# Two-layer hybrid decoder trunk: position tables called one block earlier, stream sums one block later, the last tile's matmuls in two pieces of columns

## The chip, the core and the metric

One core of one Trainium2 chip runs the whole program as one launch. The metric is the device time in microseconds; a comparison on the chip takes the median over several executions. Each engine works through its own queue of instructions in the order in which the program was built, and waits at an instruction until the semaphores that it names are reached. PE is the matrix engine, DVE the vector engine, ACT the scalar engine, POOL the general engine, SP the engine whose queue issues most DMAs.

## The reference, cut to what matters

```python
for l in range(2):                                   # h is (256 tokens, 1024)
    h = h + 0.5 * swiglu(rmsnorm(h, ffn1_norm[l]), ffn1_w_gate[l], ffn1_w_up[l], ffn1_w_down[l])
    u = rmsnorm(h, mix_norm[l])
    z = u @ w_in[l]                                  # latent attention | differential attention | pooling | gates
    ...                                              # three mixers; RoPE and ALiBi use `positions`
    h = h + merged @ w_out[l]
    h = h + 0.5 * swiglu(rmsnorm(h, ffn2_norm[l]), ffn2_w_gate[l], ffn2_w_up[l], ffn2_w_down[l])
return rmsnorm(h, final_norm)
```

`swiglu` is `(silu(x @ w_gate) * (x @ w_up)) @ w_down` with an inner width of 2816. All is float32.

## The kernel before

**Products.** A float32 product is made of three products of rounded parts: every operand is split into `hi` (rounded) and `lo` (the rest), and `mm3` issues hi·hi, hi·lo and lo·hi into one PSUM tile (lines 212 to 214; the second one, line 213, is the first that needs `lo` of the weights). Weights come in tiles of 128 x 4 x 512 (1 MB) by DMAs from SP's queue into five `raw` buffers. ACT casts a tile to `hi` (line 194), DVE subtracts to get `lo` (line 195), each into three buffers; a `raw` buffer is free for the next DMA when its `lo` is done. PE uses a weight tile in 24 matmuls of 512 columns: 4 slices of k, 2 token tiles `t`, 3 parts.

**A feed-forward stage** (`ffn`) walks over the inner width in blocks of 512 columns, c = 0, 512, 1024, 1536, 2048, 2560. A block has a gate half (m = 0) and an up half (m = 1), each of two weight tiles. Counted from 0, weight tiles 0 to 3 belong to block 0, tiles 4 and 5 to the gate half and 6 and 7 to the up half of block 512, 8 to 11 to block 1024, 12 to 15 to block 1536. `turned` transposes the product of the block before (line 428) between the gate and the up half. One block of each stage (c = 2048 in the first stage, 1536 in the three others; `sevens`) is done with seven products instead of eight (`Seven`). It needs sums and differences of the activations, made on DVE and ACT by `stream` (lines 240 to 250), and differences of weights, made on DVE by `sums` (line 258).

**Position tables.** `tables` makes the RoPE and ALiBi tables once, in the first stage. POOL writes a token value into two tiles, `pi` and `pr` (lines 525, 526), which ties the two DMAs behind it to the product `g` that is handed over; then ACT's queue issues the DMAs (lines 527, 528): `pi` gathers 256 single integers, two per partition, `pr` copies the same 1 KB row to 128 partitions. DVE turns them into `ndist` and `ang` (lines 536 to 569), ACT into sines. A third DMA, `lr` (line 578), reuses the buffer of `pr`. The tables are first read in the mixing stage.

**The end.** In the last stage `gemm_tokens` is called with `tail=2`: the last two weight tiles of w_down are done for token tile 0 first and then for token tile 1. For each token tile, `last_half` then adds to h (line 500), squares (ACT, 952), multiplies with the norm's weights (954), takes the power -1/2 on POOL (959), scales columns 0 to 511 on DVE (960) and 512 to 1023 on ACT (962), and stores them by a DMA of SP's and one of ACT's queue.

The order on each engine is set by a scheduler of the framework when the program is built, and the framework puts in the semaphore waits: for data, for buffers, and for tiles that overlap.

Of the kernel before, what the change touches and what calls it, by code (L numbers as in the profile page):

```python
# [11 lines left out]
F32 = mybir.dt.float32  # L12
# [3 lines left out]
AF = mybir.ActivationFunctionType  # L16
# [80 lines left out]
def trunk(ctx, tc, x, xt, positions, wall, small, lamrow, fnorm, out):  # L97
# [110 lines left out]
            split(slice(k, k + step))  # L208
        return hi, lo

    def mm3(ps, lh, ll, rh, rl, start, stop):
        nc.tensor.matmul(ps, lhsT=lh, rhs=rh, start=start, stop=False)  # L212
        nc.tensor.matmul(ps, lhsT=lh, rhs=rl, start=False, stop=False)  # L213
        nc.tensor.matmul(ps, lhsT=ll, rhs=rh, start=False, stop=stop)  # L214

    flat = lambda a: a.rearrange("p k n -> p (k n)")

# [97 lines left out]
            add(c21, c, m1)  # L315
            return (a, u2), (c21, m5)

    def gemm_tokens(specs, xh, xl, n, before=None, tail=1, early=None):

        ps = [acc(), acc()]
        last = specs[-1][2] + specs[-1][3] - 1
        parts = [[s] for s in specs[:-tail]] + [specs[-tail:]]
        for part in parts:
            w = [(s[2] + j, hi[:, j, :], lo[:, j, :]) for s in part for hi, lo in (wsplit(s),) for j in range(s[3])]
            if before and part is parts[-1]:
                before()
# [5 lines left out]
            for k, wh, wl, t in order:  # L334
                tk = slice(t * P, (t + 1) * P)
                mm3(ps[t][:, :n], xh(k)[:, tk], xl(k)[:, tk], wh, wl, k == 0, k == last)
        return ps

    def rsqrt_mean(dst, src, n):
# [4 lines left out]
    class Norm:  # L344
# [73 lines left out]
    def ffn(l, pre, u, following, midway=None):  # L418
# [18 lines left out]
        pending = None  # L437
        for c in range(0, DFF, 512):
            n = min(512, DFF - c)
            if c == 1024 and midway:  # L440
                midway(g[0][:, :2])
            spec = lambda b, k: (f"{pre}_gu", l, k, 4, b, 512)
            if c == 0:

                ps = [[b() for _ in range(2)] for b in (acc, trp)]
                for k0 in (0, 4):
                    for m in range(2):
                        wh, wl = wsplit(spec(m * 512, k0))
# [10 lines left out]
                if sevens(l, pre)[0] == 1024:  # L459
                    seven.stream(u.hi, u.lo)  # L460
            elif c in sevens(l, pre):
                rows = seven.run(lambda: turned(*pending))
                ps = [[rows[t][m] for t in range(2)] for m in range(2)]
            elif n == 512:
                ps = []
                if c + 512 in sevens(l, pre):
                    at = 2 * c + 1024
                    last = latest[0]
                    seven.sums([spec(at, 0), spec(at + 512, 0), spec(at + 512, 4), spec(at, 4)])
                    latest[0] = last  # L470
                for m in range(2):
                    ps.append(gemm_tokens([spec(2 * c + m * 512, k) for k in (0, 4)], u.xh, u.xl, 512))
# [19 lines left out]
            pending = c, g  # L492
        nxt = following() if following else None
        for half in range(2):
            pd = gemm_tokens([(f"{pre}_w_down", l, k, min(4, KF - k), half * 512, 512) for k in range(0, KF, 4)],
                             lambda k: ghi[k // 8][:, k % 8, :], lambda k: glo[k // 8][:, k % 8, :], 512,
                             tail=1 if nxt else 2, early=(lambda: turned(*pending)) if half == 0 else None)
            for t in range(2):
                hs = h[:, t, half * 512:(half + 1) * 512]
                nc.vector.scalar_tensor_tensor(out=hs, in0=pd[t], scalar=0.5, in1=hs, op0=ALU.mult, op1=ALU.add)  # L500
            if nxt:
                nxt.half(half)
            elif l == DEPTH - 1 and pre == "ffn2":
                last_half(half)
        return nxt


# [430 lines left out]

    hf = {}

    def last_half(n):
        if n == 0:
            hf["fn"] = big([P, D], F32, "fn")
            nc.scalar.dma_start(out=hf["fn"], in_=fnorm.broadcast_to([P, D]))
            hf["ss"] = sp.tile([P, 2, 2], F32, tag="ss", name="ss", bufs=2)
            hf["o"] = big([P, 2, D], F32, "of")
            hf["r"] = sp.tile([P, 2], F32, tag="r", name="r", bufs=2)
        ss, o, r = hf["ss"], hf["o"], hf["r"]
        ns = slice(n * 512, (n + 1) * 512)
        for t in range(2):  # L950
            sq = tp.tile([P, 512], F32, tag="C", name="sq")
            nc.scalar.activation(out=sq, in_=h[:, t, ns], func=AF.Square, accum_out=ss[:, n, t:t + 1])
            rt, s_ = r[:, t:t + 1], ss[:, n, t:t + 1]
            nc.vector.tensor_tensor(out=o[:, t, ns], in0=h[:, t, ns], in1=hf["fn"][:, ns], op=ALU.mult)
            if n == 0:
                nc.vector.tensor_scalar(out=rt, in0=s_, scalar1=1.0 / D, scalar2=EPS, op0=ALU.mult, op1=ALU.add)
                continue
            nc.vector.scalar_tensor_tensor(out=rt, in0=s_, scalar=1.0 / D, in1=rt, op0=ALU.mult, op1=ALU.add)
            nc.gpsimd.tensor_tensor(out=rt, in0=rt, in1=mhalf[:, :1], op=ALU.pow)
            nc.vector.tensor_scalar(out=o[:, t, :512], in0=o[:, t, :512], scalar1=rt, scalar2=None, op0=ALU.mult)  # L960
            nc.sync.dma_start(out=out[t * P:(t + 1) * P, :512], in_=o[:, t, :512])
            nc.scalar.activation(out=o[:, t, 512:], in_=o[:, t, 512:], func=AF.Identity, scale=rt)
            nc.scalar.dma_start(out=out[t * P:(t + 1) * P, 512:], in_=o[:, t, 512:])

    u = Norm(0, SM_F1)
    u.first(0)
# [71 lines left out]
```

## Time and profile before

| | |
|---|---|
| median of 3 runs (lowest to highest) | 1209.01 us (1208.99 to 1210.8) |
| the profiled execution's own time | 1208.78 us |
| its span, first to last instruction | 1207.0 us |
| PE busy | 1193.4 us (99%) |
| DVE / ACT / POOL busy | 818.9 (68%) / 603.4 (50%) / 68.2 us (6%) |
[...]
| chain that ended last | PE 88%, DVE 5%, issue 4%, DMA 2% |

The profiled execution lies 0.23 us under the median, and its time 1.78 us over its span. A matmul's record is longer than the distance to the next one, since matmuls are pipelined: distances are read from start to start. In a timeline row the first two numbers are start and duration in microseconds, and the brackets say how long the engine had been idle before and what released it.

### The profile page before, as it was taken

How to read it: one execution, taken by the hardware profiler on the slowest of the kernel's cores; microseconds unless marked ns; L12 is line 12 of the kernel's file. 1: busy time of each engine (PE TensorE's matmuls, PEld its weight loads, DVE VectorE, ACT ScalarE, POOL GpSimd, SP SyncE). 2: the span in 40 equal slices, each digit the busy share in tenths (PEclk: the TensorE clock that was granted, in tenths of full speed). 3: DMA queues.
4: the chain of work that ended last, by engine and by line, in shares of the span. 5: the costliest groups of instructions: out<-in, count | busy, mean ns of one | idle time of the engine just before them, and what ended most of it. 6: DMA issues, size and time to landing. Idle time of an engine off the chain costs nothing.

```text
span 1207.0 us, 14974 instructions
## 1 busy us (share of the span) xinstructions
PE 1193.4 (99%) x5944; PEld 999.8 (83%) x5944; DVE 818.9 (68%) x1124; ACT 603.4 (50%) x792; POOL 68.2 (6%) x126
## 2 busy tenths in 40 slices
PE   9999999999999999999999999999999999999997
PEld 7878889997788888888888888899877888888886
DVE  6789646777757658963558964568686485599553
ACT  6456444545644455643445643455455445446432
POOL 0000000600100000000000000034010000000000
PEclk9999999999999999999999999999999999999999
DMA  9645545235455554655554565544433554545540
GB/s 338 261 179 177 213 166 204 83 136 179 140 174 180 176 201 141 211 193 186 184 204 172 176 225 175 179 148 147 146 137 140 177 205 170 180 175 211 177 153 35
DMA packets 35478, 212.86 MB, mean 176 GB/s; under 512 B 4177, under 2 KB 5585, under 8 KB 12113
## 3 DMA queue, kind: packets, MB, share of 16 engines
q1 hardware_dynamic: 34272, 210.52, 49.8%
q10 hardware_dynamic: 1136, 1.40, 0.4%
q8 instruction: 46, 0.75, 0.2%
q14 instruction: 24, 0.19, 0.0%
HBM read 210.85 MB, written 1.05 MB: 176 GB/s over the span
## 4 chain that ended last, share of the span: by engine, by line
PE 88%; DVE 5%; issue 4%; DMA 2%; ACT 1%; POOL 0%; SPq 0%; POOLq 0%; ACTq 0%; DVEq 0%
PE acc L212 24%; PE acc L213 23%; PE acc L214 23%; PE acc L278 6%; PE o L772 2%; PE tr L428 1%; DVE lo L195 1%; PE tr L738 1%; PE tr L765 1%; PE tr L214 1%; PE tr L212 1%; PE tr L213 1%; PE tr L727 1%; DMA raw<-wall 1%; PE tr L359 1%
## 5 line engine op out<-in xcount | busy, mean ns | idle before, releaser
L195 DVE TENSOR_TENSOR lo<-raw,hi 128x1024 fp32r<-128x1024 f32 (+4 forms) x274 | 428.9, 1580 | 281.9 <-ACT hi L194 281.7
L194 ACT CAST hi<-raw 128x1024 fp32r<-128x1024 f32 (+4 forms) x274 | 358.0, 1330 | 375.3 <-PE acc L214 274.4
L212 PE MATMUL acc<-hi,uhi 128*128 128x512 f32 (+1 forms) x768 | 300.9, 392 | 0.5 <-DVE uhi L376 0.5
L213 PE MATMUL acc<-lo,uhi 128*128 128x512 f32 (+1 forms) x768 | 299.0, 389 | 2.3 <-DVE lo L195 2.3
L214 PE MATMUL acc<-hi,ulo 128*128 128x512 f32 (+1 forms) x768 | 298.2, 389 | 0.4 <-DVE ulo L377 0.4
L213 PEld LDWEIGHTS acc<-lo,uhi 128*128 128x128 f32 x768 | 144.3, 188 | 31.1 <-DVE lo L195 2.7
L212 PEld LDWEIGHTS acc<-hi,uhi 128*128 128x128 f32 x768 | 144.0, 188 | 30.0 <-issue 2.2
L214 PEld LDWEIGHTS acc<-hi,ulo 128*128 128x128 f32 x768 | 144.1, 188 | 29.4 <-DVE ulo L377 1.0
L212 PE MATMUL acc<-hi,ghi 128*128 128x512 f32 x352 | 137.7, 391 | 0.0
L213 PE MATMUL acc<-lo,ghi 128*128 128x512 f32 x352 | 137.4, 390 | 0.0
L214 PE MATMUL acc<-hi,glo 128*128 128x512 f32 x352 | 137.3, 390 | 0.0
L212 PEld LDWEIGHTS acc<-hi,ghi 128*128 128x128 f32 x352 | 66.1, 188 | 13.8
L214 PEld LDWEIGHTS acc<-hi,glo 128*128 128x128 f32 x352 | 66.1, 188 | 13.6
L213 PEld LDWEIGHTS acc<-lo,ghi 128*128 128x128 f32 x352 | 66.1, 188 | 13.4
L757 ACT ACTIVATE e<-e,mx 128x128 f32<-128x128 f32 (+1 forms) x96 | 42.7, 446 | 56.0 <-DVE mx L753 34.1
L212 PE MATMUL acc<-uhi,hi 128*128 128x256 f32 x192 | 55.6, 290 | 0.0
L213 PE MATMUL acc<-ulo,hi 128*128 128x256 f32 x192 | 55.2, 288 | 0.0
L214 PE MATMUL acc<-uhi,lo 128*128 128x256 f32 x192 | 55.0, 288 | 0.0
L342 POOL TENSOR_TENSOR r<-r,mhalf 128x2 f32<-128x2 f32 x6 | 4.2, 701 | 699.8 <-DVE r L341 699.8
L222 ACT CAST hi<-raw 128x2048 fp32r<-128x2048 f32 x16 | 30.8, 1923 | 20.8 <-PE acc L214 19.9
L488 ACT ACTIVATE sg<-acc,r 128x512 f32<-128x512 f32 (+1 forms) x44 | 28.4, 652 | 24.6 <-PE acc L214 24.5
L212 PE MATMUL acc<-hi,y 128*128 128x512 f32 x96 | 37.8, 393 | 0.0
(236 smaller groups left out, 1639.6 us busy)
## 6 DMA issues: line engine op xcount, KB each, us to landing
raw<-wall SPq DMA_DIRECT2D x182, 1024.0 KB, 4.9
raw<-wall SPq DMA_DIRECT2D x26, 256.0 KB, 5.4
raw<-wall SPq DMA_DIRECT2D x10, 512.0 KB, 3.6
raw<-wall SPq DMA_DIRECT2D x4, 832.0 KB, 4.4
raw<-wall SPq DMA_DIRECT2D x2, 768.0 KB, 4.3
xT<-xt SPq DMA_DIRECT2D x8, 128.0 KB, 4.3
h<-x SPq DMA_DIRECT2D x4, 256.0 KB, 5.9
fn<-fnorm ACTq DMA_DIRECT2D x1, 512.0 KB, 4.8
```

The source lines that it names most:

```text
L194: nc.scalar.copy(out=hif[:, ks], in_=rawf[:, ks])
L195: nc.vector.tensor_tensor(out=lof[:, ks], in0=rawf[:, ks], in1=hif[:, ks].bitcast(F32), op=ALU.subtract)
L212: nc.tensor.matmul(ps, lhsT=lh, rhs=rh, start=start, stop=False)
L213: nc.tensor.matmul(ps, lhsT=lh, rhs=rl, start=False, stop=False)
L214: nc.tensor.matmul(ps, lhsT=ll, rhs=rh, start=False, stop=stop)
L222: nc.scalar.copy(out=flat(hi), in_=flat(x))
L278: nc.tensor.matmul(ps, lhsT=x, rhs=y, start=not onto and k == 0 and n == 0, stop=k == 3 and n == 2, skip_group_check=onto)
L359: nc.tensor.transpose(out=ps[:, (i * 2 + t) * P:(i * 2 + t + 1) * P], in_=h[:, t, k * P:(k + 1) * P], identity=ident)
L428: nc.tensor.transpose(out=ptr[:, (i * 2 + t) * P:(i * 2 + t + 1) * P], in_=g[t][:, (j + i) * P:(j + i + 1) * P], identity=ident)
L488: nc.scalar.activation(out=sg, in_=ps[0][t], func=AF.Silu, scale=r)
L757: nc.scalar.activation(out=e[:, sl], in_=e[:, sl], func=AF.Exp, bias=mx[:, i:i + 1], scale=-(2.0 ** -(hd + 1)) if slope else -1.0, accum_o ...
L772: nc.tensor.matmul(o[:, hd * 64:(hd + 1) * 64], lhsT=eT[:, j * P:(j + 1) * P], rhs=v[:, kt, hd * 64:(hd + 1) * 64], start=(kt == 0), stop= ...
```

## The change

Three edits. `tables` is called at the start of block 512 and not of block 1024, so that it hangs on the product of block 0. In the first stage `stream` is called in block 1024 and not in block 512 (`c + 1024 == sevens(l, pre)[0]`; in the other stages this is block 512 as before). And in the last half of the last stage, the final two weight tiles are done as three pieces: token tile 0 with 512 columns, token tile 1 with columns 0 to 255, then token tile 1 with columns 256 to 511; `done` is called after each, so that the addition to h, the squares and the multiplication follow each piece. The scaling of the output is cut at column 640 instead of 512.

```diff
-    def gemm_tokens(specs, xh, xl, n, before=None, tail=1, early=None):
+    def gemm_tokens(specs, xh, xl, n, before=None, tail=1, early=None, done=None):
...
-        last = specs[-1][2] + specs[-1][3] - 1
+        ends = [specs[-1][2] + specs[-1][3] - 1] + ([specs[-tail][2] - 1] if done else [])
...
+            if part is parts[-1] and done:
+                pieces = [(0, slice(0, n)), (1, slice(0, n // 2)), (1, slice(n // 2, n))]
+            else:
+                pieces = [(None, slice(0, n))]
+            for piece, cols in pieces:
+                for k, wh, wl, t in order:
+                    if piece in (None, t):
+                        tk = slice(t * P, (t + 1) * P)
+                        mm3(ps[t][:, cols], xh(k)[:, tk], xl(k)[:, tk], wh[:, cols], wl[:, cols], k == 0,
+                            k in ends, piece is not None)
+                if piece is not None:
+                    done(ps[piece], piece, cols)
...
-            if c == 1024 and midway:
+            if c == 512 and midway:
                 midway(g[0][:, :2])
...
-                        if c == 512 and not seven.sh:
+                        if c + 1024 == sevens(l, pre)[0]:
                             seven.stream(u.hi, u.lo)
...
+            def added(bank, t, cols):
+                hs = h[:, t, half * 512 + cols.start:half * 512 + cols.stop]
+                nc.vector.scalar_tensor_tensor(out=hs, in0=bank[:, cols], scalar=0.5, in1=hs, op0=ALU.mult, op1=ALU.add)
+
+            def ended(bank, t, cols):
+                added(bank, t, cols)
+                last_piece(t, half * 512 + cols.start, half * 512 + cols.stop)
...
+    def last_piece(t, c0, c1):
...
+        sq = tp.tile([P, 512], F32, tag="C", name="sq")
+        nc.scalar.activation(out=sq[:, :c1 - c0], in_=h[:, t, c0:c1], func=AF.Square, accum_out=s_)
+        nc.vector.tensor_tensor(out=o[:, t, c0:c1], in0=h[:, t, c0:c1], in1=hf["fn"][:, c0:c1], op=ALU.mult)
...
+        if c1 == D:
             nc.gpsimd.tensor_tensor(out=rt, in0=rt, in1=mhalf[:, :1], op=ALU.pow)
...
+            cut = 640
+            nc.vector.tensor_scalar(out=o[:, t, :cut], in0=o[:, t, :cut], scalar1=rt, scalar2=None, op0=ALU.mult)
+            nc.sync.dma_start(out=out[t * P:(t + 1) * P, :cut], in_=o[:, t, :cut])
+            nc.scalar.activation(out=o[:, t, cut:], in_=o[:, t, cut:], func=AF.Identity, scale=rt)
+            nc.scalar.dma_start(out=out[t * P:(t + 1) * P, cut:], in_=o[:, t, cut:])
```

**ACT's queue in block 512.** In the kernel before, these rows stand there: the last two of the four casts of weight tile 5 (128x512 each), the whole casts of weight tiles 6 and 7 (128x2048), a Silu, and the cast of weight tile 8.

```order
L194 CAST hi<-raw 128x512 [waits DMAHW3_49]
L194 CAST hi<-raw 128x512 [waits DMAHW4_49]
L194 CAST hi<-raw 128x2048 [waits DMAHW5_49,DVE_49,PE_49]
L194 CAST hi<-raw 128x2048 [waits DMAHW6_49,DVE_49,PE_49]
L488 ACTIVATE sg<-acc,r 128x512 [waits DVE_49,PE_49]
L194 CAST hi<-raw 128x2048 [waits DMAHW7_49,DVE_49,PE_49]
```

In the changed kernel the same place reads:

```order
L194 CAST hi<-raw 128x512 [waits DMAHW3_49]
L194 CAST hi<-raw 128x512 [waits DMAHW4_49]
L544 DMA pi<-positions 128x2x1 [waits Pool_49]
L545 DMA pr<-positions 128x256 [waits Pool_49]
L194 CAST hi<-raw 128x2048 [waits DMAHW5_49,DVE_49,PE_49]
L595 DMA lr<-lamrow 128x256 [waits DMAHW7_49,DVE_49]
L194 CAST hi<-raw 128x2048 [waits DMAHW0_49,PE_49,Activation_49]
L496 ACTIVATE sg<-acc,r 128x512 [waits PE_49]
L194 CAST hi<-raw 128x2048 [waits DMAHW1_49,PE_49,Activation_49]
```

The two position DMAs now stand ahead of the cast of weight tile 6, and the `lr` DMA, which waits for `pr` to land and for DVE to have read it, ahead of the cast of weight tile 7.

**DVE's queue in block 512.** In the kernel before, the products `g` of block 0, the last two pieces of `lo` of weight tile 5 and the `lo` of weight tiles 6 to 8 follow one another:

```order
L490 SCALAR_TENSOR_TENSOR g<-tr,r,sg 128x512 x2
L195 TENSOR_TENSOR lo<-raw,hi 128x512 x2
L195 TENSOR_TENSOR lo<-raw,hi 128x2048 x3
```

In the changed kernel, from the last two pieces of weight tile 5 to the `lo` of weight tile 6 (the rows for `ci`, `pf` and `cf` read `pi`; those for `ri` read `pr`):

```order
L571 CAST pf<-pi 128x2
L555 CAST cf<-ci 128x4
L575 TENSOR_SCALAR ang<-sm,pf 128x16 x2
L553 TENSOR_SCALAR ri<-pr 128x256
L554 TENSOR_SCALAR ri<-pr 128x256
L577 TENSOR_SCALAR kk<-ang 128x32
L555 CAST rf<-ri 128x512
L579 TENSOR_SCALAR kk<-kk 128x32
...
L562 SCALAR_TENSOR_TENSOR ndist<-part 128x256
L561 TENSOR_TENSOR part<-part 128x256
L584 SCALAR_TENSOR_TENSOR ang<-kk,ang 128x32
L195 TENSOR_TENSOR lo<-raw,hi 128x2048
```

From `ri` on, thirteen table operations stand ahead of the `lo` of weight tile 6 (the dots stand for five more `part` rows); there were none.

**PE's queue at the end.** In the changed kernel the last matmul of the piece with columns 0 to 255 and the first of the piece with columns 256 to 511 (both of token tile 1, in one PSUM tile) read:

```order
L214 MATMUL acc<-hi,glo 128x256
L212 MATMUL acc<-hi,ghi 128x256 [waits DVE_49]
L213 MATMUL acc<-lo,ghi 128x256
L214 MATMUL acc<-hi,glo 128x256
L212 MATMUL acc<-hi,ghi 128x256
```

The wait for DVE is new. It goes away when the addition to h after the first column piece is left out, so it is the wait for that addition, which reads the other half of the same PSUM tile. On DVE that addition stands here:

```order
L969 TENSOR_TENSOR of<-h,fn 128x512
L973 SCALAR_TENSOR_TENSOR r<-ss_9209,r 128x1
L977 TENSOR_SCALAR of<-of,r 128x640
L505 SCALAR_TENSOR_TENSOR h<-acc,h 128x256
L969 TENSOR_TENSOR of<-h,fn 128x256
```

It is the fourth row, behind the output scaling of token tile 0 (`of`, 640 columns).

## Rows read from the trace of the kernel before

**Rows 1.** Who waited for whom, PE: us in total, times, longest.

```profile
PE acc L213 <- DVE lo L195: 2.3, 1, 2.3
```

**Rows 2.** Timeline of PE, weight tile 6 and weight tile 13.

```profile
41.28 0.39 PE L213 MATMUL acc<-lo,uhi 128*128 128x512 f32 x1
41.50 0.39 PE L214 MATMUL acc<-hi,ulo 128*128 128x512 f32 x1
...
82.69 0.50 PE L213 MATMUL acc<-lo,uhi 128*128 128x512 f32 x1 [2.27 <-DVE lo L195]
```

**Rows 3.** Timeline of DVE in the first stage.

```profile
29.47 1.41 DVE L490 SCALAR_TENSOR_TENSOR g<-tr,r,sg 128x512 f32<-128x512 f32 x2
30.79 1.29 DVE L195 TENSOR_TENSOR lo<-raw,hi 128x512 fp32r<-128x512 f32 x2
32.44 2.29 DVE L195 TENSOR_TENSOR lo<-raw,hi 128x2048 fp32r<-128x2048 f32 x1 [0.36 <-ACT hi L194]
...
59.15 0.29 DVE L536 TENSOR_SCALAR ri<-pr 128x256 int32<-128x256 int32 x1 [2.41 <-DMA pr<-positions]
...
61.90 0.42 DVE L538 CAST rf<-ri 128x512 f32<-128x512 int32 x1
...
62.38 0.35 DVE L540 TENSOR_SCALAR part<-rf,cf 128x256 f32<-128x256 f32 x1
...
64.43 0.38 DVE L558 TENSOR_SCALAR ang<-sm,pf 128x16 f32<-128x16 f32 x1
...
80.35 4.48 DVE L195 TENSOR_TENSOR lo<-raw,hi 128x2048 fp32r<-128x2048 f32 x2
```

**Rows 4.** Chain that ended last, 53 to 60 us: start, us, what.

```profile
53.47 5.59 DMA pr<-positions
```

**Rows 5.** Timeline of POOL and of ACT, first stage.

```profile
50.65 0.58 POOL L525 COPY pi<-g 128x2 int32<-128x2 int32 x1 [26.54 <-DVE g L490]
...
51.26 0.39 ACTq L527 DMA_DIRECT2D pi<-positions  x1
...
68.94 1.28 ACT L488 ACT_TABLE_LOAD   x1
```

**Rows 6.** DMA issues in 20 to 100 us: KB, us to landing.

```profile
lr<-lamrow ACTq DMA_DIRECT2D x1, 128.0 KB, 3.0
pi<-positions ACTq DMA_DIRECT2D x1, 1.0 KB, 2.1
```

**Rows 7.** DMA queues (packets, MB, share): 55.5 to 58.5, 52 to 53.2, 31.95 to 39.7 us.

```profile
q1 hardware_dynamic: 121, 0.87, 71.7%
q10 hardware_dynamic: 142, 0.13, 15.4%
...
q10 hardware_dynamic: 272, 0.00, 10.5%
...
q1 hardware_dynamic: 450, 3.29, 101.6%
```

**Rows 8.** Timeline of DVE and ACT at the end.

```profile
1198.66 0.49 DVE L960 TENSOR_SCALAR of<-of,r 128x512 f32<-128x512 f32 x1 [0.66 <-POOL r L959]
...
1200.43 0.69 DVE L500 SCALAR_TENSOR_TENSOR h<-acc,h 128x512 f32<-128x512 f32 x1 [1.28 <-PE acc L214]
...
1202.74 0.72 ACT L962 ACTIVATE of<-of,r 128x512 f32<-128x512 f32 x1 [0.86 <-POOL r L959]
...
1203.49 0.35 ACTq L963 DMA_DIRECT2D out<-of  x1
```

**Rows 9.** Instructions of tiles g and sq: ns min/median/max, forms.

```profile
L490 DVE SCALAR_TENSOR_TENSOR g<-acc,r,sg x32: 476/745/751, 49.8 to 1140.6; 128x512 f32<-128x512 f32 x24, 128x256 f32<-128x256 f32 x8
...
L614 ACT ACTIVATE sq<-acc x8: 276/332/385, 201.2 to 800.6; 128x256 f32<-128x256 f32 x4, 128x128 f32<-128x128 f32 x4
```

**Rows 10.** Timeline of PE, matmuls of 256 columns in the mixing stage.

```profile
203.72 0.28 PE L213 MATMUL acc<-ulo,hi 128*128 128x256 f32 x1
203.83 0.28 PE L214 MATMUL acc<-uhi,lo 128*128 128x256 f32 x1
```

More of the change, by code (lines that the diff above doesn't have):

```diff
@@ L209, in wsplit_now, with mm3 @@
         return hi, lo
[L211 to L214, printed above, removed]
+    def mm3(ps, lh, ll, rh, rl, start, stop, onto=False):
+        nc.tensor.matmul(ps, lhsT=lh, rhs=rh, start=start, stop=False, skip_group_check=onto)
+        nc.tensor.matmul(ps, lhsT=lh, rhs=rl, start=False, stop=False, skip_group_check=onto)
+        nc.tensor.matmul(ps, lhsT=ll, rhs=rh, start=False, stop=stop, skip_group_check=onto)
     flat = lambda a: a.rearrange("p k n -> p (k n)")
@@ L333, in gemm_tokens @@
                 order.sort(key=lambda o: o[3])
-            for k, wh, wl, t in order:
-                tk = slice(t * P, (t + 1) * P)
-                mm3(ps[t][:, :n], xh(k)[:, tk], xl(k)[:, tk], wh, wl, k == 0, k == last)
+            if part is parts[-1] and done:
[10 more added lines that the diff above has]
+                    done(ps[piece], piece, cols)
         return ps
@@ L458, in ffn @@
                 seven = Seven(u.xh, u.xl)
-                if sevens(l, pre)[0] == 1024:
-                    seven.stream(u.hi, u.lo)
             elif c in sevens(l, pre):
@@ L494, in ffn @@
         for half in range(2):
+            def added(bank, t, cols):
[4 more added lines that the diff above has]
+                last_piece(t, half * 512 + cols.start, half * 512 + cols.stop)
             pd = gemm_tokens([(f"{pre}_w_down", l, k, min(4, KF - k), half * 512, 512) for k in range(0, KF, 4)],
                              lambda k: ghi[k // 8][:, k % 8, :], lambda k: glo[k // 8][:, k % 8, :], 512,
-                             tail=1 if nxt else 2, early=(lambda: turned(*pending)) if half == 0 else None)
+                             tail=1 if nxt else 2, early=(lambda: turned(*pending)) if half == 0 else None,
+                             done=ended if half and not nxt else None)
             for t in range(2):
-                hs = h[:, t, half * 512:(half + 1) * 512]
-                nc.vector.scalar_tensor_tensor(out=hs, in0=pd[t], scalar=0.5, in1=hs, op0=ALU.mult, op1=ALU.add)
+                if nxt or half == 0:
+                    added(pd[t], t, slice(0, 512))
+                if not nxt and half == 0:
+                    last_piece(t, 0, 512)
             if nxt:
                 nxt.half(half)
-            elif l == DEPTH - 1 and pre == "ffn2":
-                last_half(half)
         return nxt
@@ L939, in trunk @@
     hf = {}
-    def last_half(n):
-        if n == 0:
+    def last_piece(t, c0, c1):
+        if not hf:
             hf["fn"] = big([P, D], F32, "fn")
             nc.scalar.dma_start(out=hf["fn"], in_=fnorm.broadcast_to([P, D]))
-            hf["ss"] = sp.tile([P, 2, 2], F32, tag="ss", name="ss", bufs=2)
+            hf["ss"] = sp.tile([P, 4], F32, tag="ss4", name="ss4", bufs=1)
             hf["o"] = big([P, 2, D], F32, "of")
             hf["r"] = sp.tile([P, 2], F32, tag="r", name="r", bufs=2)
[L948 to L957, printed above, removed]
+        o, rt, s_ = hf["o"], hf["r"][:, t:t + 1], hf["ss"][:, t:t + 1]
+        sq = tp.tile([P, 512], F32, tag="C", name="sq")
+        nc.scalar.activation(out=sq[:, :c1 - c0], in_=h[:, t, c0:c1], func=AF.Square, accum_out=s_)
+        nc.vector.tensor_tensor(out=o[:, t, c0:c1], in0=h[:, t, c0:c1], in1=hf["fn"][:, c0:c1], op=ALU.mult)
+        if c0 == 0:
+            nc.vector.tensor_scalar(out=rt, in0=s_, scalar1=1.0 / D, scalar2=EPS, op0=ALU.mult, op1=ALU.add)
+        else:
@@ L958, in last_half @@
             nc.vector.scalar_tensor_tensor(out=rt, in0=s_, scalar=1.0 / D, in1=rt, op0=ALU.mult, op1=ALU.add)
+        if c1 == D:
             nc.gpsimd.tensor_tensor(out=rt, in0=rt, in1=mhalf[:, :1], op=ALU.pow)
-            nc.vector.tensor_scalar(out=o[:, t, :512], in0=o[:, t, :512], scalar1=rt, scalar2=None, op0=ALU.mult)
-            nc.sync.dma_start(out=out[t * P:(t + 1) * P, :512], in_=o[:, t, :512])
-            nc.scalar.activation(out=o[:, t, 512:], in_=o[:, t, 512:], func=AF.Identity, scale=rt)
@@ L963, in last_half @@
-            nc.scalar.dma_start(out=out[t * P:(t + 1) * P, 512:], in_=o[:, t, 512:])
+            cut = 640
[3 more added lines that the diff above has]
+            nc.scalar.dma_start(out=out[t * P:(t + 1) * P, cut:], in_=o[:, t, cut:])
     u = Norm(0, SM_F1)
```

## The prediction

> **What bounds the kernel now.** I read the page first: PE is busy for 99% of the span at full granted clock, and the chain that ended last lies on PE for 88%. So only two things can move the time: a stretch in which PE waits, and the work behind PE's last matmul. The list of PE's waits names one of size, 2.3 us for `lo` of a weight tile [rows 1]. PE's timeline puts it at weight tile 13, where line 213 starts at 82.69 after 2.27 us of idle time [rows 2]. DVE's timeline shows why: DVE does the `lo` of tiles 13 and 14 from 80.35 on, as soon as it gets to them [rows 3]; it is late, not starved. Going back along DVE, it stood idle for 2.41 us before `ri` at 59.15, for the `pr` DMA [rows 3], which the chain shows as 5.59 us from its issue at 53.47 [rows 4]. With the table operations behind that wait and the stream sums ahead of it, DVE never caught up. The end: the last addition to h starts at 1200.43, the ACT part of the output is issued at 1203.49 [rows 8], and the span ends at 1207.0.
>
> So the change can win at most these 2.27 us in the first stage, 0.19% of the time, and a few tenths at the end.
>
> **Tables a block sooner: where the wait goes.** What is late next is read from the order: the same wait for `pr` now stands on DVE ahead of the `lo` of tile 6. In the kernel before, that `lo` started at 32.44 and ended at 34.7 [rows 3], and PE needed it at 41.28 [rows 2]: 6.5 us of cover. Step by step:
>
> The first of the two products `g` of block 0 is ready at about 30.2 (29.47 plus half of 1.41) [rows 3]. From POOL's copy to the issue of `pi` took 50.65 to 51.26 [rows 5], so `pi` is issued at about 30.9. Alone it landed in 2.1 us [rows 6]. But it will not be alone: q1, the queue of SP with the weights, moved 450 records between 31.95 and 39.7, 28 for each of the 16 DMA engines, one every 0.28 us, without a pause (101.6% is two in flight) [rows 7]. Tiles 8 to 10 keep it so until about 40; they are issued as before, only tile 11 waits for the `lo` of tile 6.
>
> How does q10, ACT's queue, fare beside it? Two DMAs of one shape tell: `lr` landed in 3.0 us [rows 6], `pr` in 5.59 beside one weight tile [rows 4]. That is 2.6 us more for 9 records per engine (128 + 16 over 16 engines), 0.29 us each, the distance of one weight record; and in that stretch q1 put through 121 records and q10 142 [rows 7]. I read this as turns, one record of each. `pi` has 272 records [rows 7], 17 per engine, because it gathers single integers: 2.1 + 17 x 0.28 = 6.9 us, done at 37.8. `pr` stands behind it in the same queue and needs another 2.9 us for its records beside weights (nearly all of 55.5 to 58.5) [rows 7], and about half a microsecond until DVE goes on (59.06 after 58.5): 41.2. I take 41.0, since the weights run out at about 40 and the last turns are quicker.
>
> [...]
>
> Then thirteen operations ahead of the `lo` of tile 6: `ri` twice (0.29 each, overlapping, 0.5), `rf` (0.42), seven of `part` and `ndist` as from 62.38 to 64.43 (2.05), three small ones (an estimate of 0.3): 3.25 us [rows 3]. The `lo` itself is 2.2 (half of 4.48) [rows 3], and PE started 0.04 after it in the old stall. 41.0 + 3.25 + 2.2 + 0.04 = 46.5, against 41.28: **PE stalls 5.2 us at tile 6.** Bounds: none, if `pr` landed as fast as `lr` did alone; 6.4, if the first record of `pi` came a microsecond later beside weights.
>
> **Does the old stall go?** After tile 6 both engines start together. DVE has until tile 13: seven `lo`, three weight differences, one sum and one `lo` of the stream, twelve operations at about 2.2 (26.5); four stream differences and four `glo` at 0.6 to 0.65 (5.0); two products at 0.7 (1.4); the remaining small table operations (an estimate of 2): 35 us. PE has 7 tiles of 24 matmuls at 0.225 (41.28 to 41.50) [rows 2], 37.8 us, and eight transposes. So DVE has about 3 us to spare, where it lacked 2.27. ACT gets one more table load, 1.28 us [rows 5], and the `lr` DMA holds its queue until `ri` is done; both fit into the 3 us. **-2.27 us.** The stream sums a block later belong to this: they lie in the same 35 us, and nothing reads them before c = 2048. The costs of mm3's new argument and of the other stages, whose order is unchanged, are nothing.
>
> **The end.** The order shows a new wait: the first matmul of columns 256 to 511 waits for the addition of columns 0 to 255, and on DVE that stands behind the scaling of token tile 0, which waits for POOL and started at 1198.66 [rows 8]. Scaling 640 columns instead of 512 makes 0.49 about 0.56, so the addition starts at about 1199.15, takes 0.48 (the 256-column minimum) [rows 9], and PE goes on at 1199.65. PE would otherwise have been there at about 1198.3: token tile 1 begins at 1196.2 (1200.43 less 18 x 0.225 and 0.2 for the last one's end), and the first piece's 18 matmuls are spaced 0.12 [rows 10]. The second piece: 18 x 0.12, 0.2 for the restart and 0.16 for the last one's end, 1202.2, where the addition started at 1200.43 before [rows 8]: 1.77 late. The shorter operations give back 0.21 (addition, 0.69 to 0.48), 0.24 (squares, 0.63 to 0.39) [rows 9] and about 0.1 (ACT's scaling, 384 of 512 columns of 0.72) [rows 8]; DVE's longer scaling then ends level with ACT's. **+1.2 us**, bounds +0.8 and +1.6. If PE did not wait, it would be -0.35: 36 x 0.12 against 18 x 0.225 on PE, less those 0.55.
>
> [...]
>
> **Sum.** Against the profiled execution's own time: 1208.78 - 2.27 + 5.2 + 1.2 = 1212.9, and 0.23 more to stand beside the median: **1213.1 us**, 0.34% slower.
>
> **The rivals.**
> 1. *`pi` goes through in bursts, `pr` lands at its own pace; no slower.* `pr` is issued at 31.5 to 32.1, when POOL's second copy is done beside the last pieces of tile 5 (30.79 plus 1.29) [rows 3], and lands after the 5.6 us of before: 37.1 to 37.7. The stall at tile 6 is 1.3 to 1.9, less than the one removed: 1208.78 - 2.27 + 1.6 + 1.2 + 0.23 = 1209.5, no change. For it speaks that 5.6 is a measured landing beside weights; against it that only one weight tile ran beside `pr`, with `pi` long done. It decides when `pr` lands before about 39.3 (a stall under 3.5). [...]
> 2. *The cover holds.* If `pr` lands by 35.8, as in the 3.0 us of `lr`, PE does not wait at all: 1207.9; with no wait at the end either, 1206.4. Against it speaks the full q1.
> 3. *DVE is late again at tile 13 or earlier.* The 3 us to spare are a sum of estimates. If ACT's queue (the wait for `lr`'s issue, the extra table load, `le` behind DVE) eats them, part of 2.27 comes back: 1214 to 1215.4.
>
> **How the numbers follow.** A measurement of this kernel tells about 0.2%, 2.4 us, from no change. The forecast gets 0.62, rival 1 0.26, rival 2 0.04, rival 3 0.08. The forecast alone spans 1211.5 to 1214.7 (stall 4.0 to 6.4, end 0.8 to 1.6). The range must take in rival 1: 1208.9 to 1215.0. Slower by over 2.4 us: the forecast without its low edge of 0.03, and rival 3: 0.67. Same: rival 1, that edge and half of rival 2, 0.31. Faster: the other half, 0.02.
>
> **What would show it.** After: PE's waits name `lo` of line 195 once, for about 5 us near 41, and not near 82. DVE stands idle before `ri` for some 4 to 8 us, with `pr` landing 9 us after its issue, and `pi` some 7 after its own. At the end PE has a gap of 1.3 us that the addition to h releases, and the last addition starts some 4.7 us later in the span than before (-2.27 + 5.2 + 1.77), near 1205. `pr` landing in under 7 us, a second PE wait between 50 and 100, or no gap at the end would each make a step wrong.

## The result and the profile after

The changed kernel takes 1216.11 us (median of 4 executions, 1215.49 to 1216.55); the kernel before took 1209.9 us beside it (4 executions, 1208.99 to 1210.8). The ratio is 1.005, 95% interval 1.0034 to 1.0066: slower by some 6 us. The forecast was 1213.1, from 1208.9 to 1215.0: the direction is right, the size is not.

The profiled execution after took 1216.55 us with a span of 1214.5; the one before took 1208.78 with 1207.0. So 7.77 us are to be found. First, PE's waits in the changed kernel (us in total, times, longest):

```profile
PE acc L213 <- DVE lo L195: 5.5, 1, 5.5
PE acc L212 <- DVE h L505: 1.1, 1, 1.1
```

One wait for `lo` is there as before [rows 1], but it is longer, and there is a new one for `h`. PE's timeline says where the first stands, and what comes behind it:

```profile
41.28 0.48 PE L212 MATMUL acc<-hi,uhi 128*128 128x512 f32 x1
47.31 0.79 PE L213 MATMUL acc<-lo,uhi 128*128 128x512 f32 x1 [5.55 <-DVE lo L195]
47.90 0.63 PE L214 MATMUL acc<-hi,ulo 128*128 128x512 f32 x1
48.33 0.63 PE L212 MATMUL acc<-hi,uhi 128*128 128x512 f32 x1
...
52.60 0.60 PE L213 MATMUL acc<-lo,uhi 128*128 128x512 f32 x1
53.02 0.41 PE L214 MATMUL acc<-hi,ulo 128*128 128x512 f32 x1
53.27 0.40 PE L212 MATMUL acc<-hi,uhi 128*128 128x512 f32 x1
```

It is weight tile 6, as foreseen, and the stall is 5.55 us. But look at the starts behind it: 47.90, 48.33, ... 0.43 us apart until 53.02, where they stood 0.22 apart before [rows 2]. The table by stretches gives the reason (length, then the busy time of PE, of its weight loads, of DVE, ACT and POOL, each with its count, then the granted clock, the DMA share and GB/s):

```profile
46.00:48.00 2.00, 0.69 (x2) 0.59 (x3) 2.00 (x5) 0.84 (x1) 0.34 (x1) 0.55 0.00 0
48.00:50.00 2.00, 2.00 (x6) 1.56 (x5) 2.00 (x2) 0.00 (x0) 0.19 (x1) 0.50 0.70 254
50.00:52.00 2.00, 2.00 (x6) 1.57 (x5) 2.00 (x5) 1.13 (x3) 0.00 (x0) 0.50 1.06 336
52.00:54.00 2.00, 2.00 (x8) 1.53 (x8) 2.00 (x9) 1.97 (x5) 0.00 (x0) 0.74 0.85 348
54.00:56.00 2.00, 2.00 (x10) 1.66 (x9) 2.00 (x3) 1.97 (x3) 0.00 (x0) 1.00 0.95 373
```

PE shows as fully busy, yet does 6 matmuls in 2 us and not 10: the granted clock is 0.50 for some 6 us after PE had restarted. The column of busy time does not show this; the count beside it and the clock do. The 13 matmuls from 47.31 to 53.02 take 5.71 us; at the spacing of [rows 2] they would take 13 x 0.225 = 2.9, and 0.1 more for the restart (41.55 to 41.90 in all_early, below): 2.7 us lost. The 0.50 stands behind 5.55 us of idle time; behind the 2.27 us in the kernel before, the clock is 1.00 (82 to 90 us). Whether the idle time is what lowers it, the filled kernels below test.

Why PE stood still is on DVE's timeline and in the DMA issues (KB, us to landing):

```profile
40.78 0.17 DVE L553 TENSOR_SCALAR ci<-pi 128x2 int32<-128x2 int32 x1 [7.48 <-DMA pi<-positions]
...
41.59 0.29 DVE L553 TENSOR_SCALAR ri<-pr 128x256 int32<-128x256 int32 x1
...
44.98 2.28 DVE L195 TENSOR_TENSOR lo<-raw,hi 128x2048 fp32r<-128x2048 f32 x1
```

```profile
pr<-positions ACTq DMA_DIRECT2D x1, 128.0 KB, 9.3
lr<-lamrow ACTq DMA_DIRECT2D x1, 128.0 KB, 2.9
pi<-positions ACTq DMA_DIRECT2D x1, 1.0 KB, 9.0
```

DVE stood 7.48 us before `ci`; `pi`, 1 KB, took 9.0 us where it took 2.1 before [rows 6], and `pr` landed 0.7 us after it (issued at 31.72 and 32.16). Without that wait the same operations and the `lo` would have ended at about 39.8 (an estimate: 44.98 + 2.28 - 7.48), ahead of 41.76, when PE ran out of work. The queues from 31.8 to 35 us, then from 35 to 40 (packets, MB, share):

```profile
q1 hardware_dynamic: 193, 1.38, 102.4%
```

```profile
q1 hardware_dynamic: 260, 1.88, 90.7%
q10 hardware_dynamic: 341, 0.07, 7.3%
```

For the first 3 us ACT's queue, q10, moves nothing at all; then its records are spread over five microseconds among the weights'. Sums over 16 engines can't tell turns from bursts, but the order of the single records in this trace can: of the 210 records of 4 bytes that q10 started from 35 to 39 us, 189 are followed within 4 to 8 ns by the start of an 8 KB record of the weights. (Shift the moment by 20 ns, and only 55 are.) That is one record of `pi`, then one of the weights.

The end, on the engines' timeline of the changed kernel:

```profile
1202.58 0.69 DVE L505 SCALAR_TENSOR_TENSOR h<-acc,h 128x512 f32<-128x512 f32 x1 [7.16 <-PE acc L214]
...
1205.35 0.42 DVE L505 SCALAR_TENSOR_TENSOR h<-acc,h 128x256 f32<-128x256 f32 x1
...
1205.82 0.38 PE L212 MATMUL acc<-hi,ghi 128*128 128x256 f32 x1 [1.13 <-DVE h L505]
...
1208.27 0.42 DVE L505 SCALAR_TENSOR_TENSOR h<-acc,h 128x256 f32<-128x256 f32 x1 [1.63 <-PE acc L214]
```

and three more rows that the accounts need beside it: the first matmul of weight tile 4, in the changed kernel and in the kernel before, and the addition of token tile 0 in the kernel before:

```profile
29.60 0.39 PE L212 MATMUL acc<-hi,uhi 128*128 128x512 f32 x1
...
29.28 0.39 PE L212 MATMUL acc<-hi,uhi 128*128 128x512 f32 x1
...
1196.35 0.69 DVE L500 SCALAR_TENSOR_TENSOR h<-acc,h 128x512 f32<-128x512 f32 x1 [7.17 <-PE acc L214]
```

The accounts of the 7.77 us. Weight tile 4 began at 29.60 after and at 29.28 before: 0.32, ahead of anything that the change moves. Stall at tile 6: 5.55. Half clock: 2.7. Old stall gone: -2.27. Together 6.30; the addition of token tile 0 is 1202.58 - 1196.35 = 6.23 later. From there to the last addition it is 5.69 us after and 4.08 before ([rows 8] has 1200.43): 1.61 more; from the last addition to the span's end 6.23 after and 6.57 before: 0.34 less. The remaining 0.27 lies outside the span (2.05 after, 1.78 before).

### The profile page after: what moved, and what is told of

Read it like the earlier page. It is cut to its first block, busy times and chain, and to the rows that moved or that the text cites. A ratio compares the mean times of both kernels' runs of the same rounds, so it can differ in the third digit from the quotient of the medians.

```text
span 1214.5 us, 15016 instructions
## 1 busy us (share of the span) xinstructions
PE 1196.7 (99%) x5962; PEld 1002.9 (83%) x5962; DVE 819.2 (67%) x1127; ACT 606.1 (50%) x795; POOL 65.8 (5%) x126
## 3 DMA queue, kind: packets, MB, share of 16 engines
q10 hardware_dynamic: 1136, 1.27, 0.3%
## 4 chain that ended last, share of the span: by engine, by line
PE 90%; DVE 3%; issue 2%; DMA 2%; ACT 1%; SPq 0%; POOL 0%; POOLq 0%; ACTq 0%; DVEq 0%
PE acc L212 25%; PE acc L213 24%; PE acc L214 24%; PE acc L278 6%; PE o L789 2%; PE tr L438 2%; PE tr L755 1%; PE tr L782 1%; PE tr L213 1%; DVE lo L195 1%; PE tr L214 1%; PE tr L212 1%; PE tr L744 1%; DMA raw<-wall 1%; PE tr L369 1%
## 5 line engine op out<-in xcount | busy, mean ns | idle before, releaser
L212 PE MATMUL acc<-hi,ghi 128*128 128x512 f32 (+1 forms) x358 | 138.8, 388 | 1.1 <-DVE h L505 1.1
L213 PE MATMUL acc<-lo,ghi 128*128 128x512 f32 (+1 forms) x358 | 138.4, 387 | 0.0
L214 PE MATMUL acc<-hi,glo 128*128 128x512 f32 (+1 forms) x358 | 138.4, 387 | 0.0
L223 DVE TENSOR_TENSOR lo<-raw,hi 128x2048 fp32r<-128x2048 f32 x16 | 36.6, 2285 | 4.0 <-ACT hi L222 4.0
```

The costliest lines, as they stand in the source:

```text
L223: nc.vector.tensor_tensor(out=flat(lo), in0=flat(x), in1=flat(hi).bitcast(F32), op=ALU.subtract)
```

## The experiments

Times are medians; ratios are to the kernel before, run on the same chip beside each of them, with the 95% interval behind them.

### The parts alone

All three start from the kernel before. *stage_only* has the two edits of the first stage:

```diff
-            if c == 1024 and midway:
+            if c == 512 and midway:
...
-                        if c == 512 and not seven.sh:
+                        if c + 1024 == sevens(l, pre)[0]:
```

*tail_only* has all the rest of the change, the end, and neither of these; *stream_only* has the second of these two edits alone.

> The kernel before with the two edits of the first stage alone (tables at c = 512, stream sums at c = 1024), the end as before. If the two halves of the change add up as I read the changed kernel's trace (a stall of 5.5 us at weight tile 6, some 2.7 us at half clock behind it, the old 2.27 us gone), it is 6.0 us slower than before, about 1215.5 to 1216, with the granted clock at 0.5 for some 6 us after the stall. Rival: the half clock comes from something else (the end's edit, chance), then there is 3.3 us of loss and the clock stays at 1.00.

> The kernel before with the edit of the end alone. My term for the end: PE has a gap of about 1.2 us before the second piece of columns, and the time is 1.2 to 1.3 us longer than before, about 1211.1; the old stall of 2.3 us at weight tile 13 is there as before. Rival: the gap is covered by the shorter last operations, and the time is as before or 0.35 us shorter.

> The kernel before with the stream sums alone moved, from c = 512 to c = 1024; tables and end as before. If the idle time of DVE before ri makes the old stall, the move alone does not take it away: DVE then has the 9 us of stream sums and the tables in one block, and the stall at weight tile 13 or before it is 2.3 us or longer, up to 5, the time 0 to 3 us above before. Rival: the move is what frees DVE; then the stall of 2.3 us goes and the time is 2.3 us under before.

stage_only: 1214.21, ratio 1.0037 (1.0025 to 1.005). The stall is there (5.2), the clock of all five executions 0.996. tail_only: 1211.81, ratio 1.001 (1.0001 to 1.0018). In its trace token tile 0's addition and the last one stand 5.69 apart, as in the changed kernel, and PE has the gap:

```profile
PE acc L213 <- DVE lo L195: 2.1, 1, 2.1
PE acc L212 <- DVE h L507: 1.1, 1, 1.1
```

So both halves cost, they add up within their uncertainty, and the half clock belongs to the first stage. stage_only's 3.9 us fall short of the expected 6.0: in part because the median of before is itself raised here (1210.31, see the last section), in part because 1214.21 itself lies 1.3 us under what I had expected, with a stall 0.4 us shorter than in the changed kernel. stream_only: 1209.77, ratio 0.9997 (0.9988 to 1.0006), with a wait of 2.0 us still at weight tile 13:

```profile
82.60 0.80 PE L213 MATMUL acc<-lo,uhi 128*128 128x512 f32 x1 [2.02 <-DVE lo L195]
```

The move of the stream sums alone does nothing. That the old stall goes when DVE no longer waits for `pr` in that block is shown by transfers_sooner below; the tables' move without that of the stream sums wasn't run.

### Which transfer, and which wait

Five kernels move the transfers. *loads_early*: the changed kernel with `pi` and `pr` issued on ACT's queue when the last slice of xT has landed; *all_early*: with `lr` too, all on POOL's queue; *only_pr_late* and *only_pi_late*: as all_early, but one transfer issued where the change has it. The core of all_early:

```diff
+    pi0 = const.tile([P, 2], I32, name="pi0")
+    pr0 = ndist[:, 1, :].bitcast(I32)
+    lr0 = mask
+    def loaded():
+        nc.gpsimd.tensor_copy(out=pi0, in_=xT[:, KD - 1, :2].bitcast(I32))
+        nc.gpsimd.dma_start(out=pi0, in_=positions.rearrange("b (t p) -> (b p) t", p=P))
...
-        nc.scalar.dma_start(out=pi, in_=positions.rearrange("b (t p) -> (b p) t", p=P))
-        nc.scalar.dma_start(out=pr, in_=positions.broadcast_to([P, S]))
+        nc.gpsimd.tensor_copy(out=pi, in_=pi0)
+        nc.gpsimd.tensor_copy(out=pr, in_=pr0)
```

> The changed kernel, but the two transfers of positions are issued some 15 us sooner, behind the last slice of xT, into spare places; POOL copies them on where they were issued before, so that the table operations keep their place. If the transfers behind the weights are what holds lo of weight tile 6, DVE has the lo done before PE needs it: no stall of PE at tile 6, none at tile 13, granted clock 1.00 throughout, and only the end's 1.2 us remain: 1208.8 less 2.3 plus 1.3, about 1207.8 to 1208.9 in the median, 7.5 to 8 us under the changed kernel. Rival: the table operations themselves are too many for the place (3.3 us of them and 2.2 of the lo); then a stall of 2 us or more stays at tile 6. Second rival: the 272 single-integer records, moved among the first weights, hold these up, and up to 2 us come back as waits before 30 us.

loads_early: 1217.49, ratio 1.0055 (1.0041 to 1.0068). Missed: the stall is 6.34 us. `pi` and `pr` no longer wait; `lr` does, in the same place. DVE's waits and timeline:

```profile
DVE lpr L606 <- DMA lr<-lamrow: 3.1, 1, 3.1
```

```profile
34.27 1.41 DVE L498 SCALAR_TENSOR_TENSOR g<-tr,r,sg 128x512 f32<-128x512 f32 x2
...
43.43 0.29 DVE L606 TENSOR_TENSOR lpr<-lr 128x128 f32<-128x128 f32 x1 [3.09 <-DMA lr<-lamrow]
...
43.73 0.69 DVE L195 TENSOR_TENSOR lo<-raw,hi 128x512 fp32r<-128x512 f32 x1
```

The `lo` behind it, the last quarter of tile 5, is what PE waits for. And `g` of block 0 came at 34.27, where it came at 30.70 in the changed kernel: the opening slipped. The traces show the 1.7 us that ACT's queue waited to issue the two transfers and, behind it, the last two loads of h issued at 19.67 and 21.49, against 15.15 and 16.75 in the changed kernel; which of the changes cost the opening wasn't tried. I had named a loss of the opening as second rival, by the records of `pi` among the first weights.

> The changed kernel with the three transfers pi, pr and lr issued on POOL's queue behind the last slice of xT (about 14 us), into pi's copy, ndist and mask as homes, so that no table operation on DVE waits for a transfer and ACT's queue issues none of them. If waits on transfers that stand ahead of lo on DVE are what costs the time in the first stage, there is no stall at weight tiles 5 or 6, none at 9 or 13, the clock stays at 1.00, and 1.2 us of the end remain: about 1 us under the kernel before, 7 us under the changed kernel. Rival: DVE has too much to do in this stretch whatever lands when; then a stall of 2 us or more stays somewhere between 38 and 90 us and the time is at or above that of the kernel before.

all_early: 1212.65, ratio 1.0022 (1.0013 to 1.0031), 3.5 us under the changed kernel, not 7. DVE waits for no transfer now, but a stall is left:

```profile
41.55 0.51 PE L213 MATMUL acc<-lo,uhi 128*128 128x512 f32 x1 [3.35 <-DVE lo L195]
41.90 0.40 PE L214 MATMUL acc<-hi,ulo 128*128 128x512 f32 x1
```

The opening is late again (`g` at 34.34; the loads of h landed 8.3 us after their issue, 6.7 in the changed kernel), and the table operations stand ahead of the last quarter of tile 5 (its `lo` at 40.82). So the rival is right in part: with all data there, the table work of about 5 us still has no room in this place once the opening slips by 3.6. That the transfers made it slip here is read from the landings; it wasn't tried by itself, and in loads_early, as late, the loads of h landed 4.4 us after their (later) issue. So neither kernel shows the changed kernel with its transfers early and its opening in place.

> As the kernel with all three transfers early, but pr is issued where the change issues it. If pi's 272 single-integer records are what made the landing so late, pr alone lands in about 5.6 us beside the weights, at 37 to 38, and the stall at weight tile 6 is 2 us or less at full clock, the time 1 to 2 us above that of the kernel with all early. If pr itself takes 9 us behind the weights, the stall is 5 us again and the time that of the changed kernel, about 6 us above before.

> As the kernel with all three transfers early, but pi is issued where the change issues it. If pi's records take turns with the weight records, pi lands 7 to 9 us after its issue, at 39 to 41, and the stall at weight tile 6 is 4 to 5.5 us with half clock behind it, 6 us above before. If pi is quick by itself (2.1 us as in the kernel before), there is no stall and the time is that of the kernel with all early.

only_pr_late: 1216.14, ratio 1.0052 (1.0038 to 1.0065); only_pi_late: 1215.85, ratio 1.0051 (1.0038 to 1.0063). Their DMA issues:

```profile
pr<-positions ACTq DMA_DIRECT2D x1, 128.0 KB, 6.8
```

```profile
pi<-positions ACTq DMA_DIRECT2D x1, 1.0 KB, 8.8
```

`pi` alone takes 8.8, as in the changed kernel. `pr` alone takes 6.8, not 5.6, and since `g` and with it the issue came later (33.28), it landed at 40.0. DVE stood 4.7 us before `ri` in the first and 6.0 us before `ci` in the second, and PE 5.27 and 5.52 us. Either one alone is enough to hold the `lo` of tile 6. I had expected a stall of 2 us for `pr` alone; that was wrong.

*transfers_sooner* takes the other way, on the kernel before: `pi` and `pr` are issued at c = 512, on POOL's queue, and all table operations stay at c = 1024.

```diff
+            if c == 512 and midway:
+                midway[0](g[0][:, :2])
             if c == 1024 and midway:
-                midway(g[0][:, :2])
+                midway[1](g[0][:, :2])
```

> The kernel before with the two halves of the tables taken apart: the transfers of pi and pr are issued (on POOL's queue) where the changed kernel issues them, at c = 512, and the table operations stay at c = 1024, behind two small copies on POOL. Stream sums and end as before. If the old stall of 2.3 us at weight tile 13 came from DVE's 2.4 us of idle time before ri, that idle time goes and the stall with it: 2.3 us under the kernel before, clock 1.00 throughout, and nothing at tile 6, since no operation of DVE waits there. Rival: DVE's own work before tile 13 is too long by itself; then 1 us or more of the stall stays and the time is within 1 us of before.

1206.39, ratio 0.9972 (0.9961 to 0.9983): 3.8 us under before. `pi` takes 6.0 and `pr` 7.5 us beside the weights, and nobody waits. DVE's waits from 30 to 90 us, and PE at weight tile 13:

```profile
DVE lo L195 <- ACT hi L194: 8.7, 3, 4.6
DVE ci L547 <- POOL pi L538: 0.3, 1, 0.3
```

```profile
79.62 0.39 PE L212 MATMUL acc<-hi,uhi 128*128 128x512 f32 x1
80.04 0.50 PE L213 MATMUL acc<-lo,uhi 128*128 128x512 f32 x1
```

The 2.4 us before `ri` and the stall behind them are gone; the span is 2.5 us shorter than before (1204.5). So DVE's wait for the transfer was the cause of the old stall. For the new one that is read from the changed kernel's trace (7.48 us of waiting, and the estimate of 39.8 without it); the runs with early transfers, whose opening slipped, don't show it by themselves.

### The half clock

*filled* puts 20 extra matmuls (results thrown away) on PE ahead of weight tile 6; *fill_short* puts 7.

```diff
+            if part is parts[0]:
+                for i in range(fill):
+                    nc.tensor.matmul(ps[0], lhsT=xh(0)[:, :P], rhs=w[0][1], start=True, stop=True)
```

> The changed kernel with 20 extra matmuls of 512 columns (results thrown away) on PE just ahead of weight tile 6, 4.5 us of work inside the stall of 5.5 us. If the stall is what lowers the granted clock, the stall now shows as about 1 us of waiting, PE goes on at the same moment (about 47.3) but at full clock, and the time is 2.7 us less than that of the changed kernel, about 1213.4. Rival: the clock falls there for another reason; then the half clock and the time stay as in the changed kernel, 1216.1.

> The changed kernel with 7 extra matmuls of 512 columns (results thrown away) ahead of weight tile 6, 1.6 us of work, few enough that DVE's order stays nearly as it is in the changed kernel: PE stands idle for about 3.9 us in place of 5.5 and goes on at the same moment. If what follows the stall at half clock is a cost of its own, the executions in which the clock stays at its higher level (mean 0.998 or 0.999) take 2.5 to 2.7 us less than the changed kernel, about 1213.5, and those in which it falls (0.995 to 0.996) about 1216. Rival: DVE is late behind tile 6 anyway, so that PE waits at tile 9 or 10 for what it gains; then the time is 1216 at either clock.

filled: 1217.21, ratio 1.0062 (1.0049 to 1.0074). In its profile the clock stays at 1.00, as I had expected; the time doesn't fall. PE's timeline:

```profile
47.78 0.50 PE L213 MATMUL acc<-lo,uhi 128*128 128x512 f32 x1 [1.47 <-DVE lo L195]
...
67.16 0.50 PE L213 MATMUL acc<-lo,uhi 128*128 128x512 f32 x1 [2.77 <-DVE lo L195]
```

A second stall of 2.77 us took the gain. But the extra matmuls had also changed the order in which DVE's work was laid out: the stream sums (55.05 to 64.16) now stood ahead of the `lo` of tile 9 (64.82; 59.06 in the changed kernel). fill_short: 1216.59, ratio 1.0055 (1.0043 to 1.0068); here `pi` and `pr` landed 9.6 and 10.5 us after issue, the stall was 6.65 us, and the clock fell all the same (0.77 in the mean from 45 to 60 us). It settles nothing. So one pair more, with DVE's order held: *order_held* ties the start of the stream sums to the `lo` of tile 9 and issues their last part behind the block's second product; *order_held_filled* adds the 20 matmuls.

```diff
+            nc.vector.tensor_copy(out=uf[:, 0, :1], in_=newest[0][:, 0, :1].bitcast(F32))
...
+                    if m == 1 and seven.sf is not None:
+                        seven.rest()
```

> The changed kernel with DVE's order fixed behind weight tile 6: the stream sums start only when the lo of weight tile 9 is done (one copied number ties them), and their last part is issued after the second product of the block. The control for the next run: the stall at weight tile 6 and the half clock behind it as in the changed kernel, no second stall, the time within 0.5 us of the changed kernel, about 1216.

> The same with 20 extra matmuls of 512 columns (results thrown away) ahead of weight tile 6; DVE's order is that of the control but for one operation. If the half clock is a cost of its own, which comes from PE standing idle and not from DVE, PE goes on at the moment of the control, at full clock, waits nowhere behind it, and the time is 2.5 to 2.7 us under the control. Rival: DVE is late behind tile 6 whatever PE's clock is; then a second wait of about 2.7 us takes the place of the half clock, as in the first filled kernel, and the time is that of the control.

order_held: 1216.34 (1215.5 to 1216.86), ratio 1.0055 (1.0043 to 1.0067). order_held_filled: 1214.85 (six executions, five of 1214.01 to 1215.85 and one of 1219.17), ratio 1.005 (1.0035 to 1.0065). PE's waits for `lo`, the first row from order_held, the two others from order_held_filled:

```profile
47.68 0.79 PE L215 MATMUL acc<-lo,uhi 128*128 128x512 f32 x1 [6.66 <-DVE lo L197]
...
48.16 0.50 PE L215 MATMUL acc<-lo,uhi 128*128 128x512 f32 x1 [2.13 <-DVE lo L197]
...
87.97 0.50 PE L215 MATMUL acc<-lo,uhi 128*128 128x512 f32 x1 [0.52 <-DVE lo L197]
```

The granted clock at 48 to 52 us in the one and in the other:

```profile
48.00:52.00 4.00, 4.00 (x10) 3.13 (x10) 4.00 (x8) 0.76 (x3) 0.53 (x1) 0.50 0.93 279
```

```profile
48.00:52.00 4.00, 3.84 (x17) 3.19 (x18) 4.00 (x10) 0.29 (x2) 0.53 (x1) 1.00 0.73 231
```

Ten matmuls against 17. With 2.13 us of idle time in place of 6.66 the clock stays at 1.00 where it was 0.50, so PE's idle time is what lowers it here: the mean clock was 0.995 to 0.997 in all five executions of the control, and 0.998 or 0.999 in five of the six with filling. The price in time is less sure. The filling saves 1.5 us in the medians, not 2.5 to 2.7; but the two intervals overlap, and the sixth execution (0.996, 1219.17) lies above all of the control, so that the saving isn't clear of noise. In the profiled pair PE went on 0.48 us later (48.16 against 47.68) and later waited 0.52 us for another `lo`; the spans differ by 1.2. My reading, which this pair doesn't prove: the half clock is a cost of its own, and part of it only covers that DVE is late anyway.

### The end

*tail_banks* is tail_only with the last two weight tiles' products for columns 256 to 511 in a bank of their own; *sooner_and_banks* is that and transfers_sooner together.

```diff
+            if part is parts[-1] and done:
+                spare = acc()
+                partly(ps[1], 1, slice(n // 2, n))
```

> The kernel before with the end in two pieces, but the last two weight tiles' products for the second piece go into a bank of their own, and what had gathered for these columns in the first bank is added to h ahead. If the wait of the second piece for the addition of the first is the whole cost of the end, PE has no gap there, and the time is 0.35 us under the kernel before or level with it. Rival: DVE's longer queue of short operations (one addition more) is what ends last; then the end stays 0.5 us or more above before.

> The same, with the end in two pieces of columns whose second piece has a bank of its own. The end by itself measured level with before, so I expect the time of the kernel with the sooner transfers alone, within 0.5 us, some 2 to 2.7 us under the kernel before. Rival: the order of work on DVE at the end differs and costs up to 1 us.

tail_banks: 1209.75, ratio 1.0001 (0.9992 to 1.001). PE has no gap at the end (the wait for `h` is gone from its list), and from the addition of token tile 0 to the last one it is 4.30 us: 1.39 less than with the shared bank, 0.22 more than before.

```profile
1197.62 0.69 DVE L512 SCALAR_TENSOR_TENSOR h<-acc,h 128x512 f32<-128x512 f32 x1 [3.66 <-PE acc L214]
...
1201.92 0.42 DVE L512 SCALAR_TENSOR_TENSOR h<-acc,h 128x256 f32<-128x256 f32 x1 [0.25 <-PE acc L214]
```

In the traces the wait on the shared bank is the whole cost of the end; the two intervals, of tail_only and of tail_banks, overlap. Without the wait the two pieces are worth nothing: the narrow matmuls take 0.22 more (36 of them 0.12 us apart, against 18 at 0.227), and the shorter work behind gives 0.19 back (6.38 from the last addition to the end, 6.57 before). sooner_and_banks: 1207.02, ratio 0.9976 (0.9966 to 0.9985), 0.6 us above transfers_sooner, a little over the 0.5 that I had allowed; the two intervals overlap.

## Why the prediction fell short, step by step

- **The old stall goes, -2.27: right.** No wait of PE near 82 is left, and no second one came between 50 and 100. I had counted the stream's move to it; that move alone does nothing (stream_only), and in transfers_sooner the stall goes without it.
- **The wait moves to tile 6 and is 5.2: right in place and size,** 5.55 measured. The sum inside hides two errors that cancel. `pi` landed at 40.8, not 37.8: it was issued 0.8 later than I took it, and its records began only after 35. `pr` then landed 0.7 us behind it and not 2.9: I had put its records behind those of `pi`, but most ran beside them (from 39 to 40 us, 66 of its 128 records of 1 KB among 63 of 4 bytes), while the weights ran dry. I had taken `pr` at 41.0 and it was there at 41.5. That 5.2 is so near to 5.55 is luck to that extent. From `ri` to the `lo` it is 3.4 (3.25 forecast).
- **Turns or bursts:** turns. Rival 1 wanted `pr` at its own pace behind a quick `pi`; `pi` took 9.0, and its records and those of the weights alternate (189 of 210, above). Even alone `pr` took 6.8, so rival 1's price was too low as well.
- **The end, +1.2: right.** The gap is 1.13 (1.35 forecast), the last addition 1.61 later (1.77), given back 0.34 (0.55): +1.27. The -0.35 for an end without the wait was wrong: its own terms, 36 x 0.12 less 18 x 0.225 less 0.55, make -0.28, and tail_banks, which has no wait, measured +0.03 (0.22 less 0.19).
- **The sum: here it failed.** "1208.78 - 2.27 + 5.2 + 1.2" prices the stall at tile 6 with its idle time alone. Behind it PE ran 13 matmuls at a granted clock of 0.50, a loss of 2.7 us, which stand in no term, no bound (6.4 was the stall's own) and no rival. 1212.9 and 2.7 are 1215.6; with 0.35 more stall and 0.32 of a later opening 1216.3, against 1216.55. The trace of before had one stall, of 2.27 us, with the clock at 1.00 behind it; the prediction doesn't ask whether the clock holds behind a longer one.
- **Rival 3, DVE late again:** not in the changed kernel, but nearer than I took it. Where the clock was kept up, DVE was late by 0.5 (order_held_filled), and with another order by 2.8 us (filled). That the 3 us to spare were in part those that PE lost by its clock is my reading; no run shows it by itself.

## What to carry to other kernels

Price a stall of PE with what follows it: the granted clock behind the stall, read from starts and counts and not from busy time (here 0.50 for some 6 us behind 5.55 us of stall). When a block is moved whose first operations wait for a transfer, ask what stands behind them on the engine that works in order; here it paid to send the transfers a block ahead (on POOL's queue) and to leave the operations where they were (-3.8 us in the medians, -2.5 in the profiled spans), while moving both cost 3.9 (stage_only). A small gather was no small transfer here while another queue was full: 1 KB in single integers took 2.1 us alone and 9.0 beside the weights.

## What the runs showed of the hardware, unexpected

- **The same stall lowers the clock in some executions and not in others.** Beside the experiments the kernel before was run 68 times. In 32 of these executions the mean granted clock was 0.999, median 1208.86 us; in 29 it was 0.998, median 1210.61; in 7 it was lower. In the profiled one the clock behind the 2.27 us stall stays at 1.00. In the profile of tail_banks, whose stall at tile 13 is 2.32 us, it falls. From 75 to 90 us:

```profile
75.00:90.00 15.00, 12.68 (x51) 9.96 (x50) 10.44 (x8) 4.51 (x3) 0.00 (x0) 0.89 0.37 140
```

  all_early, with 3.35 us of stall, has both: 1210.57 to 1212.09 at 0.999 (4 executions), 1211.49 to 1214.53 at 0.996 to 0.998 (7). Of the kernels with over 5 us none stayed at 0.999 (stage_only, only_pr_late, only_pi_late, loads_early: 5 executions each). What decides it in a single execution is open, and so is how long the clock stays down: with 5.27 us of stall in only_pr_late the matmuls start 0.43 us apart until 50.07 and 0.23 to 0.25 from there on, where the changed kernel still has 0.43 until 53.02. The mean clock is a rough sign, too: transfers_sooner, which has no stall, shows 0.998 in three of its seven executions, its profiled one among them, which has 1.00 in all stretches from 30 to 105 us. In the profile of the kernel before the clock is 0.50 from 1204 us on, behind PE's last matmul (which starts at 1200.00), where it costs nothing. The falls may be why transfers_sooner gains 3.8 us in the medians and 2.5 in the spans: it removes the stall, and with it the falls behind it; no trace of the kernel before with such a fall was kept.
- **A transfer's first record can start over 3 us after its issue** while another queue keeps the engines full: `pi` was issued at 31.72 and q10 moved nothing until 35, with q1 at 102%. Alone, in the kernel before, `pi` was issued at 51.26 and its first record started 1.0 us later. The difference is the larger part of what I had missed in `pi`.
